# Two-layer hybrid encoder: attention weighed with values as the stationary operand, group weights broadcast through memory, four gates computed last, scan steps paced one by one

## The chip, the cores and the metric

One core of a Trainium2 chip runs the whole program. The metric is the device time of one execution in microseconds (us), the median of three runs. PE is TensorE's matmul side and PEld its weight loads, DVE is VectorE, ACT is ScalarE, POOL is GpSimd, SP is SyncE, whose queue issues most of the transfers.

## The reference, cut to what matters

Each of the two layers is a half-step feed-forward block, a mixer and another half-step feed-forward block, on 512 positions of 1024 channels. The mixer adds three gated branches:

```
h = rmsnorm(x);  P = h @ W_in
A = gated DeltaNet, 4 heads of 128, both directions, chunks of 64   # a scan over 8 chunks
B = pooling, 4 channel groups, windows 2/4/8/16, a 128x128 map per group
C = 3 groups of 4 heads of 64, dilated windowed attention;          # o_g, lse_g for each group g
    wts = softmax over g of lse_g;  C = sum_g wts_g * o_g           # per position and head
x = x + W_o( sum_i sigmoid(h W_g_i + b_g_i) * (branch_i @ P_i) )
```

## The kernel before

Activations lie with channels on partitions and the 512 positions along the free side. A `gemm` makes 128 output channels: for each of its k-tiles of 128 input channels it runs three matmuls of 128x512 (weights and activations are each split into a high and a low part, `wh`/`wl` and `h`/`l`; the three products are lines 232, 234 and 236). Weights come by DMA on SP's queue into `raw` (three buffers), ACT copies `wh` and DVE subtracts `wl` (`split`, lines 182 and 183, four buffer pairs). A gemm on the normed input has 8 k-tiles, 24 matmuls; the projections of branches A and B (`wpa`, `wpb`) have 12 and that of branch C (`wpc`) has 6. Three PSUM banks hold gemm results (`acc`), five hold everything else (`m`).

The mixer is a row of gemms into which smaller work is threaded. `step()` is called after every gemm matmul, and two lanes count these calls: lane "d" releases a piece of the DeltaNet every 14 calls (`DPACE`), lane "a" a piece of attention every 13 or 9 calls (the numbers in `ORDER`). A chunk of the scan is `read` (16 matmul records, then eight DVE instructions, line 679), `solve` (line 699, then lines 706 and 708) and `write` (line 716, then line 726); each needs the one before it. A scheduler with priorities then fixes the order on each engine, and every engine runs its own queue in order.

`ORDER` runs the projections of attention group 0, its attention, groups 1 and 2, the pooling branch in one piece, then the eight `wpa` gemms (`y`) with the attention of group 2 among them, then `merge`. Attention works on blocks of four softmax tiles of 128 queries: `scores`, softmax, `turn` (four transposes of the probabilities into `pe`, lines 899 and 902) and `weigh` (line 914): `pe`, 128x128, is the stationary operand and 64 columns of values move past it, so the result has queries on partitions. `merge` therefore multiplies each group's result by a column of weights (line 961), transposes it on PE (line 966, 24 transposes) and adds the three. It writes group 0's weights to memory and reads them back in another order (lines 954 and 956).

Then come eight `wpb` and eight `wpc` gemms. The gates of branches B and C were computed early and stored to memory (`gd`); each gemm loads its gate tile (line 1086, on ACT's queue, four buffers `f`), DVE forms the product (line 1088) and POOL adds it to `mg[d]` (line 1089). The eight output gemms `wo` need all of `mg`, split into high and low parts.

Of the kernel before, what the change touches and what calls it, by code (L numbers as in the profile page):

```python
# [16 lines left out]
P = 128  # L17
# [79 lines left out]
def trunk(ctx: ExitStack, tc: tile.TileContext, A, out):  # L97
# [69 lines left out]
    dW = pd.tile([T, 4], F32, name="dW")  # L167
    gd = pd.tile([2 * NB, P, T], F32, name="gd")
# [36 lines left out]
    lanes = {"d": [[], 0, DPACE], "a": [[], 0, 0]}  # L205

    def step():

        for ln in lanes.values():
            if ln[0]:  # L210
                ln[1] += 1
                if ln[1] >= ln[2]:
                    ln[1] = 0
                    ln[0].pop(0)()

    def drain(k, left=0):
        while len(lanes[k][0]) > left:
            lanes[k][0].pop(0)()
# [153 lines left out]
    def deltanet(l, W):  # L372
# [175 lines left out]

        for tok in DNORD[1].split():
            {"v": values, "t": vrows, "q": queries, "n": qnorm}[tok[0]](int(tok[1]))  # L550
# [10 lines left out]
        for tok in DNORD[2].split():  # L561
            {"v": values, "t": vrows, "q": queries, "n": qnorm}[tok[0]](int(tok[1]))
        V.tensor_scalar(out=qv, in0=qv, scalar1=4 * L2_EPS, scalar2=None, op0=ALU.add)

# [77 lines left out]
        def krows(h):  # L642
# [10 lines left out]
            KD.append(kd)  # L653

# [89 lines left out]
        def out_norm():  # L744
            v = small(16, "ov", 1)
            V.tensor_scalar(out=v, in0=qv, scalar1=P * RMS_EPS, scalar2=None, op0=ALU.mult)
# [20 lines left out]
        def add(*fs):  # L767
            X.steps.append(lambda: [f() for f in fs])
# [36 lines left out]
    def attention(l, W):  # L805
# [8 lines left out]
        def project(g):  # L814
# [7 lines left out]
            for hp in range(2):  # L822
# [4 lines left out]
                p = bank()  # L827
                if g == 0:
                    p2 = bank()
                    PE.transpose(p[:64, 0:P], vf[:, 0:64], ident)  # L830
                    for s in range(1, 4):
                        PE.transpose(p[:, s * P:(s + 1) * P], vf[:, s * P - 64:s * P + 64], ident)
                    PE.transpose(p2[:64, 0:P], vf[:, 448:512], ident)
                    S.activation(vx[:64, hp * P:(hp + 1) * P], p2[:64, 0:P], AF.Copy)
                    S.activation(vt[:64, hp * P:(hp + 1) * P], p[:64, 0:P], AF.Copy)
                    o3 = vt.rearrange("p (s c) -> p s c", c=256)[:, 1:4, hp * P:(hp + 1) * P]
                    S.activation(o3, p[:, P:T].rearrange("p (s c) -> p s c", c=P), AF.Copy)
                else:
                    for r in range(4):
                        PE.transpose(p[:, r * P:(r + 1) * P], vf[:, r:T:4], ident)  # L840
                    o3 = vt.rearrange("p (s c) -> p s c", c=256)[:, :, hp * P:(hp + 1) * P]
                    S.activation(o3, p.rearrange("p (s c) -> p s c", c=P), AF.Copy)
            qkv[g] = (q, k, vt, vx)

        def attend(g):

            q, k, vt, vx = qkv[g]
            og = OG[g] = ring()
# [359 lines left out]
```

## Time and profile before

| what | value |
|---|---|
| median of 3 runs | 2594.52 us (2593.94 to 2596.76) |
| the profiled execution's own time | 2593.36 us |
| its span, first to last instruction | 2591.6 us |
| PE busy | 2565.7 us, 99% |
| DVE, ACT, POOL busy | 1469.1, 1008.9, 162.3 us |
| granted TensorE clock | 0.998 |

The difference between the execution's time and its span lies outside the instructions. Matmuls are pipelined, so the duration of one is longer than the distance to the next: what a matmul costs is read from the distance between starts.

### The profile page before, as it was taken

To read this page: it belongs to the slowest core of one execution; us is meant where nothing else is said; L and a number is where in the kernel's file an instruction comes from. 1 tells how busy PE (TensorE), PEld (TensorE's weight loads), DVE (VectorE), ACT (ScalarE), POOL (GpSimd) and SP (SyncE) were. 2 spreads that over 40 slices of the span, in tenths; PEclk is the share of its full clock that TensorE was granted. 3 is DMA by queue.
4 is the path that set the end of the run, shared out by engine and by line. 5 is a ranking of instruction groups with operands and counts; after the bars stand their busy time and mean duration, and the time that the engine had idled before them with its cause. 6 is when DMAs were issued, how large, how long until landed. Compare 5 with 4: busy or idle time off the path is not lost.

```text
span 2591.6 us, 34050 instructions
## 1 busy us (share of the span) xinstructions
PE 2565.7 (99%) x13064; PEld 2102.1 (81%) x13064; DVE 1469.1 (57%) x2698; ACT 1008.9 (39%) x1948; POOL 162.3 (6%) x117
## 2 busy tenths in 40 slices
PE   9999999999999999999999999999999999999998
PEld 7888887888887788888888888878888877888887
DVE  6444349956757754444444443599466487544433
ACT  5333234564434333333233332355644343333322
POOL 1000000000230300000000000000012203000010
PEclk9999999999999999999999999999999999999999
DMA  4223333332432522233322333323334325322232
GB/s 154 97 98 96 112 111 98 99 118 87 122 103 74 171 91 96 97 98 96 100 96 94 97 101 114 112 89 106 107 98 121 92 74 175 98 96 94 94 98 82
DMA packets 96979, 269.36 MB, mean 104 GB/s; under 512 B 15664, under 2 KB 20144, under 8 KB 96816
## 3 DMA queue, kind: packets, MB, share of 16 engines
q1 hardware_dynamic: 75280, 229.39, 28.2%
q10 hardware_dynamic: 21536, 37.80, 4.5%
q8 instruction: 102, 1.67, 0.3%
q14 instruction: 61, 0.50, 0.1%
HBM read 243.99 MB, written 16.86 MB: 101 GB/s over the span
## 4 chain that ended last, share of the span: by engine, by line
PE 95%; DVE 2%; ACT 1%; issue 1%; DMA 1%; POOL 0%; SPq 0%; DVEq 0%; ACTq 0%
PE acc L236 29%; PE acc L232 29%; PE acc L234 29%; PE m L914 1%; PE m L672 1%; PE m L699 1%; PE m L716 1%; PE m L735 1%; PE m L899 1%; PE m L869 0%; DMA raw<-in_wo_dram 0%; DVE wl L183 0%; PE m L647 0%; PE m L1023 0%; PE m L608 0%
## 5 line engine op out<-in xcount | busy, mean ns | idle before, releaser
L182 ACT ACTIVATE wh<-raw 128x512 fp32r<-128x512 f32 (+1 forms) x870 | 539.1, 620 | 1193.0 <-PE acc L234 1068.7
L234 PE MATMUL acc<-xl,wh 128*128 128x512 f32 x2400 | 941.9, 393 | 1.4 <-DVE xl L1126 1.2
L236 PE MATMUL acc<-xh,wl 128*128 128x512 f32 x2400 | 941.7, 392 | 1.4 <-DVE wl L183 1.4
L232 PE MATMUL acc<-xh,wh 128*128 128x512 f32 x2400 | 941.1, 392 | 1.3 <-ACT wh L182 1.1
L183 DVE TENSOR_TENSOR wl<-raw,wh 128x512 fp32r<-128x512 f32 (+1 forms) x870 | 606.0, 697 | 578.1 <-ACT wh L182 572.1
L232 PEld LDWEIGHTS acc<-xh,wh 128*128 128x128 f32 x2400 | 450.9, 188 | 99.1 <-issue 3.0
L234 PEld LDWEIGHTS acc<-xl,wh 128*128 128x128 f32 x2400 | 450.9, 188 | 96.9 <-DVE xl L1126 3.9
L236 PEld LDWEIGHTS acc<-xh,wl 128*128 128x128 f32 x2400 | 451.0, 188 | 96.7 <-DVE wl L183 2.3
L232 PE MATMUL acc<-r,wh 128*128 128x512 f32 x970 | 379.8, 392 | 5.8 <-DVE f L1088 4.5
L234 PE MATMUL acc<-r,wh 128*128 128x512 f32 x970 | 378.5, 391 | 3.5 <-DVE r L183 3.5
L236 PE MATMUL acc<-r,wl 128*128 128x512 f32 x970 | 377.7, 390 | 0.0
L232 PEld LDWEIGHTS acc<-r,wh 128*128 128x128 f32 x970 | 182.1, 188 | 46.5 <-ACT r L182 4.4
L234 PEld LDWEIGHTS acc<-r,wh 128*128 128x128 f32 x970 | 182.2, 188 | 42.5 <-DVE r L183 5.8
L236 PEld LDWEIGHTS acc<-r,wl 128*128 128x128 f32 x970 | 182.1, 188 | 37.5
L298 DVE TENSOR_TENSOR t<-acc,R 128x512 f32<-128x512 f32 x88 | 60.9, 692 | 132.2 <-PE acc L236 132.2
L294 DVE TENSOR_TENSOR f<-acc,R 128x512 f32<-128x512 f32 x88 | 60.9, 692 | 128.1 <-PE acc L236 128.0
L182 ACT ACTIVATE r<-t 128x512 fp32r<-128x512 f32 x96 | 60.6, 632 | 132.6 <-DVE t L299 127.4
L183 DVE TENSOR_TENSOR r<-t,r 128x512 fp32r<-128x512 f32 x96 | 66.2, 692 | 60.8 <-ACT r L182 60.8
L579 POOL MEMSET r<- 128x1024 f32 x2 | 1.9, 953 | 1107.7 <-PE acc L236 1107.7
L365 DVE SCALAR_TENSOR_TENSOR f<-t,cw,f 128x512 f32<-128x512 f32 x96 | 69.2, 741 | 0.0
L295 ACT ACTIVATE f<-f 128x512 f32<-128x512 f32 x88 | 55.6, 632 | 23.0 <-DVE f L294 22.9
L299 DVE TENSOR_TENSOR t<-t,f 128x512 f32<-128x512 f32 x88 | 60.4, 686 | 1.3 <-ACT f L295 1.3
(282 smaller groups left out, 1744.6 us busy)
## 6 DMA issues: line engine op xcount, KB each, us to landing
raw<-in_win_dram SPq DMA_DIRECT2D x76, 512.0 KB, 3.7
raw<-in_wgt_dram SPq DMA_DIRECT2D x48, 512.0 KB, 3.3
raw<-in_f2g_dram SPq DMA_DIRECT2D x44, 512.0 KB, 3.2
raw<-in_f2u_dram SPq DMA_DIRECT2D x44, 512.0 KB, 3.3
raw<-in_f1g_dram SPq DMA_DIRECT2D x43, 512.0 KB, 3.3
raw<-in_f1u_dram SPq DMA_DIRECT2D x43, 512.0 KB, 3.3
raw<-in_f1d_dram SPq DMA_DIRECT2D x32, 512.0 KB, 3.5
raw<-in_f2d_dram SPq DMA_DIRECT2D x32, 512.0 KB, 3.4
```

Of the source, the lines that this page charges most:

```text
L182: S.activation(h, raw, AF.Copy)
L183: V.tensor_tensor(out=l, in0=raw, in1=f32(h), op=ALU.subtract)
L232: PE.matmul(acc, a, h, start=(k == 0), stop=False)
L234: PE.matmul(acc, a, l, start=False, stop=False)
L236: last = PE.matmul(acc, b, h, start=False, stop=(k == nk - 1))
L294: V.tensor_tensor(out=g1, in0=g, in1=R, op=ALU.mult)
L295: S.activation(g1, g1, AF.Silu)
L298: V.tensor_tensor(out=u1, in0=u, in1=R, op=ALU.mult)
L299: V.tensor_tensor(out=u1, in0=u1, in1=g1, op=ALU.mult)
L365: V.scalar_tensor_tensor(out=a, in0=cp[:, j:j + T], scalar=w[:, j:j + 1], in1=a, op0=ALU.mult, op1=ALU.add)
L672: PE.matmul(p1[:, h * P:(h + 1) * P], KQ[h][:, c * P:(c + 1) * P], X.ST[:, di * T + h * P:di * T + (h + 1) * P], start=True, stop=True)
L699: PE.matmul(P3[di][r0:r0 + 64, h * P:(h + 1) * P], M[di][r0:r0 + 64, o:o + 64], U[b][r0:r0 + 64, di * T + h * P:di * T + (h + 1) * P], sta ...
```

## The change

- `weigh` takes a pair of blocks (even and odd heads). The values, 128x64, become the stationary operand and the probabilities, 128 columns, move. The two blocks write the two halves of the partitions, so the result has channels on partitions, and the 24 transposes of `merge` go.
- The pieces of lane "a" are fewer: two `turn`s and the next `scores` in one piece, one `weigh` for a pair, a piece every 20 calls (36 before the second). Group 2's attention starts after its projection and the third pooling gemm.
- The group weights are computed with the last `weigh`, transposed once (48x128), written to memory, and read back by six transfers that repeat each row over 64 partitions. `merge` is then seven DVE products and sums on whole tiles, without PE, at high priority.
- Four of the eight branch C gates are no longer stored early: each is computed just ahead of its `wpc` gemm. `gd` shrinks from 16 tiles to 12.
- The scan is paced with 15 calls ahead of `read`, 13 ahead of `solve` and 9 ahead of `write`, in place of 14 each. The squares of the queries (`qnorm`) move into the DeltaNet's lane.
- Pooling is split into four pieces, and the transposes of attention's values (`vrow`) wait until the next piece of a lane that comes at least 8 calls later.

```diff
-DNORD = ("k0 k1 k2 k3 E0 G0 q0 E1 G1 E2", "v0", "v1 t0 t1 v2 t2 v3 t3 n0 q1 n1 q2 n2 q3 n3")
-ORDER = "p0 a0/13 p1 p2 D a1/9 P D a2/9 y D m"
+DNORD = ("k0 k1 k2 k3 E0 G0 q0 E1 G1 E2", "v0", "v1 t0 t1 v2 t2 v3 t3 q1 q2 q3")
+
+ORDER = "p0 a0 p1 P0 P1 a1 p2 P2 a2 P3 y"
+APACE = 20
+DUE = 8
+
+NG = 4
+YORD = "10 11 12 13 14 15 16 17 20 21 22 23 24 25 26 27"
 MG = 13
-DPACE = 14
+DPACE = {"read": 15, "solve": 13, "write": 9}
...
-    dW = pd.tile([T, 4], F32, name="dW")
-    gd = pd.tile([2 * NB, P, T], F32, name="gd")
+    dW = pd.tile([48, P], F32, name="dW")
+    gd = pd.tile([NB + NG, P, T], F32, name="gd")
...
-    lanes = {"d": [[], 0, DPACE], "a": [[], 0, 0]}
+    lanes = {"d": [[], 0], "a": [[], 0]}
+
+    pend = []
+
+    def flush(due=0):
+        while pend and pend[0][0] >= due:
+            pend.pop(0)[1]()
 
     def step():
 
+        for q in pend:
+            q[0] += 1
         for ln in lanes.values():
             if ln[0]:
                 ln[1] += 1
-                if ln[1] >= ln[2]:
+                if ln[1] >= ln[0][0][0]:
                     ln[1] = 0
-                    ln[0].pop(0)()
+                    flush(DUE)
+                    ln[0].pop(0)[1]()
...
             KD.append(kd)
+            qnorm(h)
...
             if s:
-                add(lambda s=s: read(s))
-            add(lambda s=s: solve(s))
+                add(lambda s=s: read(s), n=DPACE["read"])
+            add(lambda s=s: solve(s), n=DPACE["solve"])
             if s == 5:
-                add(lambda: write(5), lambda: out_block(1), lambda: out_block(2))
+                add(lambda: write(5), lambda: out_block(1), lambda: out_block(2), n=DPACE["write"])
             elif s < 7:
-                add(lambda s=s: write(s))
-        X.rest = 4
+                add(lambda s=s: write(s), n=DPACE["write"])
+        X.rest = 5
         add(lambda: out_block(0), lambda: out_block(3))
         add(out_norm)
+        add()
...
+                pend.append([0, lambda hp=hp, vf=vf: vrow(g, hp, vf, vt, vx)])
...
-            def weigh(b, y):
-                if b.ip not in po:
-                    po[b.ip] = bank()
-                i, h, s, n = b.ks[y]
-                t_ = i + s
-                vv = vx[:n, h * 64:h * 64 + 64] if t_ == 4 else vt[:n, t_ * 256 + h * 64:t_ * 256 + h * 64 + 64]
-                o_ = (i - b.ip) * 256 + h * 64
-                PE.matmul(po[b.ip][:, o_:o_ + 64], b.pe[:n, y * P:(y + 1) * P], vv, start=(s == 0), stop=(s == kw // P - 1))
+            def weigh(pair):
+                if g not in OG:
+                    flush()
+                    OG[g] = ring()
+                og = OG[g]
+
+                ip = pair[0].ip
+                if ip not in po:
+                    po[ip] = bank()
+                for y in range(4):
+                    for b in pair:
+                        i, h, s, n = b.ks[y]
+                        t_ = i + s
+                        vv = vx[:n, h * 64:h * 64 + 64] if t_ == 4 else vt[:n, t_ * 256 + h * 64:t_ * 256 + h * 64 + 64]
+                        o_ = (h // 2) * 256 + (i - ip) * P
+                        PE.matmul(po[ip][64 * b.par:64 * b.par + 64, o_:o_ + P], vv, b.pe[:n, y * P:(y + 1) * P], start=(s == 0), stop=(s == kw // P - 1))
+                if pair[1] is [c for c in B if c.ip == ip][-1]:
+                    S.activation(og.rearrange("p (f t) -> p f t", f=2)[:, :, ip * P:(ip + 2) * P], po[ip].rearrange("p (f t) -> p f t", f=2), AF.Copy)
...
-            steps = [lambda: scores(pairs[0])]
-            for j, pair in enumerate(pairs):
-                if j + 1 < len(pairs):
-                    steps.append(lambda n=pairs[j + 1]: scores(n))
-                for b in pair:
-                    steps.append(lambda b=b: turn(b))
-                for b in pair:
-                    steps.append(lambda b=b: [weigh(b, y) for y in range(4)])
+
+            def first(j):
+                for b in pairs[j - 1] if j else []:
+                    turn(b)
+                if j < len(pairs):
+                    scores(pairs[j])
+            steps = [lambda: first(0)]
+            for j in range(len(pairs)):
+                steps.append(lambda j=j: first(j + 1))
+                steps.append(lambda j=j: weigh(pairs[j]))
+            if g == 2:
+                last = steps.pop()
+                steps.append(lambda: [weights_a(), last(), weights_b()])
...
-            nc.sync.dma_start(dW.rearrange("(m r) h -> m r h", r=4), we[:, 0:16].rearrange("p (r h) -> p r h", h=4))
-            w0 = small(16, "w0", 1)
-            nc.sync.dma_start(w0.rearrange("p (b h) -> p b h", h=4), dW.rearrange("(b p) h -> p b h", p=P))
-            for g in (1, 2, 0):
-                wcol = w0 if g == 0 else we[:, 16 * g:16 * g + 16]
-                V.tensor_tensor(out=OG[g].rearrange("p (x d) -> p x d", d=64), in0=OG[g].rearrange("p (x d) -> p x d", d=64),
-                                in1=bc(wcol, 64), op=ALU.mult)
-                for f in range(2):
-                    p = bank()
-                    for i in range(4):
-                        PE.transpose(p[:, i * P:(i + 1) * P], OG[g][:, i * 256 + f * P:i * 256 + (f + 1) * P], ident)
-                    if g == 0:
-                        V.tensor_tensor(out=yc[f], in0=p, in1=yc[f], op=ALU.add)
-                        continue
-                    yv = yc[f].rearrange("p (m r) -> p r m", r=4)
-                    pv = p.rearrange("p (r m) -> p r m", r=4)
-                    if g == 1:
-                        S.activation(yv, pv, AF.Copy)
-                    else:
-                        V.tensor_tensor(out=yv, in0=pv, in1=yv, op=ALU.add)
+            wp = WT_p[0] = small(48, "wp", 1)
+            for g in range(3):
+                V.tensor_tensor(out=wp[:, 16 * g:16 * g + 16].rearrange("p (h r) -> p r h", r=4),
+                                in0=we[:, 16 * g:16 * g + 16].rearrange("p (r h) -> p r h", h=4),
+                                in1=zz[:, 0:16].rearrange("p (r h) -> p r h", h=4), op=ALU.mult)
+
+        WT_p = [None]
+
+        def weights_b():
+
+            pw_ = bank()
+            PE.transpose(pw_[:48, 0:P], WT_p[0], ident)
+            wr = tt()
+            S.activation(wr[:48, 0:P], pw_[:48, 0:P], AF.Copy)
+            nc.sync.dma_start(dW, wr[:48, 0:P])
+            for g in range(3):
+                w = ring()
+                WT.append(w)
+                for e_ in range(2):
+
+                    src = dW[16 * g:16 * g + 16, :].rearrange("(f e r) m -> e f (r m)", f=2, e=2)[e_:e_ + 1]
+                    nc.sync.dma_start(w[64 * e_:64 * e_ + 64, :].rearrange("p (f t) -> p f t", f=2), src.to_broadcast([64, 2, T]))
+
+        def merge():
+            wT = WT
+            for g in (1, 2):
+                V.tensor_tensor(out=OG[g], in0=OG[g], in1=wT[g], op=ALU.mult)
+            V.tensor_tensor(out=OG[1], in0=OG[1], in1=OG[2], op=ALU.add)
+            yc = []
+            for f in range(2):
+                o = OG[0][:, f * T:(f + 1) * T].rearrange("p (m r) -> p m r", r=4)
+                for op, z in ((ALU.mult, wT[0]), (ALU.add, OG[1])):
+                    V.tensor_tensor(out=o, in0=o, in1=z[:, f * T:(f + 1) * T].rearrange("p (r m) -> p m r", r=4), op=op)
+                yc.append(OG[0][:, f * T:(f + 1) * T])
...
-        pw2 = tt()
-        nc.sync.dma_start(pw2, A["poolw"][l])
-        YB = []
-        for g, win in enumerate((2, 4, 8, 16)):
+
+        def pool(g):
+            win = (2, 4, 8, 16)[g]
+            pw2 = small(P, "pw2", 1)
+            nc.sync.dma_start(pw2, A["poolw"][l][:, g * P:(g + 1) * P])
...
-        for d in range(2 * NB):
+        for d in range(NB + NG):
...
-                lanes["a"][0].extend(attend(int(tok[1])))
-                lanes["a"][1:] = [0, int(tok[3:])]
-            elif tok == "D":
-                drain("a")
-            elif tok == "P":
-                YB = pooling(l, W[16:20])
-            elif tok == "m":
-                YC = merge()
+                lanes["a"][0].extend((APACE + 16 * (j == 1), f) for j, f in enumerate(attend(int(tok[1]))))
+            elif tok[0] == "P":
+                YB.append(pool(int(tok[1])))
...
-        for br, yy, wp in ((0, YB, "wpb"), (1, YC, "wpc")):
-            for d in range(NB):
-                t = tf()
-                nc.scalar.dma_start(t, gd[br * NB + d])
-                y = gemm(A[wp][l][d], yy)
-                V.scalar_tensor_tensor(out=t, in0=t, scalar=1.0, in1=y, op0=ALU.add, op1=ALU.mult)
-                G.tensor_tensor(out=mg[d], in0=mg[d], in1=t, op=ALU.add)
+        YC = None
+        for br, d in [(int(c[0]), int(c[1])) for c in YORD.split()]:
+            if br == 2 and YC is None:
+                drain("a")
+                with tc.high_priority(offset=AHEAD_E):
+                    YC = merge()
+            yy, wp = ((YB, "wpb"), (YC, "wpc"))[br - 1]
+            t = tf()
+            if br == 2 and d >= NG:
+                gate(2, d, t)
+            else:
+                nc.scalar.dma_start(t, gd[(br - 1) * NB + d])
+            y = gemm(A[wp][l][d], yy)
+            V.scalar_tensor_tensor(out=t, in0=t, scalar=1.0, in1=y, op0=ALU.add, op1=ALU.mult)
+            G.tensor_tensor(out=mg[d], in0=mg[d], in1=t, op=ALU.add)
```

On PE, at the end of the `wpa` gemms: `m` is a PSUM bank, `acc` a gemm's bank, `r` under line 914 first the probabilities and then the values. Before:

```order
L236 MATMUL acc_7226<-r_5794,wl_7228 128x512
L914 MATMUL m_7217<-r_6560,r_7071 128x64 x4
L232 MATMUL acc_7226<-r_5842,wh_7227 128x512
L234 MATMUL acc_7226<-r_5842,wh_7227 128x512
L236 MATMUL acc_7226<-r_5842,wl_7228 128x512
L232 MATMUL acc_7226<-r_5853,wh_7227 128x512
L234 MATMUL acc_7226<-r_5853,wh_7227 128x512
L236 MATMUL acc_7226<-r_5853,wl_7228 128x512
L966 MATMUL m_7274<-ident,r_6657 128x128 x4
L966 MATMUL m_7280<-ident,r_6657 128x128 x4
L966 MATMUL m_7287<-ident,r_6990 128x128 x4
```

After (line 939 is `weigh`, 246 to 250 the gemm), the same place:

```order
L939 MATMUL m_7107<-r_6945,r_6609 64x128
L939 MATMUL m_7107<-r_6954,r_6609 64x128
L939 MATMUL m_7107<-r_6945,r_6609 64x128
L939 MATMUL m_7107<-r_6954,r_6609 64x128
L939 MATMUL m_7107<-r_6945,r_6609 64x128
L939 MATMUL m_7107<-r_6954,r_6609 64x128
L939 MATMUL m_7107<-r_6945,r_6609 64x128
L939 MATMUL m_7107<-r_6954,r_6609 64x128
L996 MATMUL m_7117<-ident,wp_7103 48x128
L250 MATMUL acc_7071<-r_5851,wl_7073 128x512
L246 MATMUL acc_7071<-r_5862,wh_7072 128x512
```

The operands have changed places, the pieces of the last pair stand together, and one transpose of 48 rows stands where 24 of 128 stood.

On DVE, from the first product of the merge. Before (the `wpa` and `wpb` stages; 961, 975 and 968 are the merge, 183 the splits, 1082 and 1088 the gated products):

```order
L961 TENSOR_TENSOR r_6657<-r_6657,we_7256 128x1024
L183 TENSOR_TENSOR wl_7345<-raw_7346,wh_7344 128x512
L902 COPY r_7071<-m_7194 128x512
L1082 SCALAR_TENSOR_TENSOR mg_3961<-mg_3961,acc_7169 128x512
L1082 SCALAR_TENSOR_TENSOR mg_3999<-mg_3999,acc_7201 128x512
L183 TENSOR_TENSOR wl_7368<-raw_7369,wh_7367 128x512
L961 TENSOR_TENSOR r_5941<-r_5941,w_1301_7270 128x1024
L961 TENSOR_TENSOR r_6990<-r_6990,we_7256 128x1024
L1082 SCALAR_TENSOR_TENSOR mg_4037<-mg_4037,acc_7226 128x512
L183 TENSOR_TENSOR wl_7391<-raw_7392,wh_7390 128x512
L975 TENSOR_TENSOR r_7272<-m_7287,r_7272 128x4x128
L975 TENSOR_TENSOR r_7272<-m_7293,r_7272 128x4x128
```

After (1017, 1011 and 1012 are the merge, 188 the splits, 1137 the gated products of `wpb`):

```order
L1017 TENSOR_TENSOR r_5993<-r_5993,r_7122 128x512 x2
L1137 SCALAR_TENSOR_TENSOR f_7182<-f_7182,acc_7184 128x512
L188 TENSOR_TENSOR wl_7278<-raw_7279,wh_7277 128x512
L1137 SCALAR_TENSOR_TENSOR f_7205<-f_7205,acc_7207 128x512
L188 TENSOR_TENSOR wl_7301<-raw_7302,wh_7300 128x512
L1011 TENSOR_TENSOR r_6568<-r_6568,r_7125 128x1024
L1137 SCALAR_TENSOR_TENSOR f_7228<-f_7228,acc_7230 128x512
L188 TENSOR_TENSOR wl_7337<-raw_7338,wh_7336 128x256
L1011 TENSOR_TENSOR r_6999<-r_6999,r_7128 128x1024
L1137 SCALAR_TENSOR_TENSOR f_7251<-f_7251,acc_7253 128x512
L1012 TENSOR_TENSOR r_6568<-r_6568,r_6999 128x1024
L188 TENSOR_TENSOR wl_7354<-raw_7355,wh_7353 128x256
```

The merge's instructions now stand among the gated products and weight splits of the `wpb` stage, and the last two of them are operands of the first `wpc` gemm.

On SP's queue, the weight loads of the `wpc` stage after the change (before, eight `wpc` loads stood in a row, then the `wo` loads):

```order
L204 DMA raw_7389<-in_wpc_dram 128x256
L204 DMA raw_7405<-in_wgt_dram 128x1024
L204 DMA raw_7442<-in_wpc_dram 128x256
L204 DMA raw_7458<-in_wgt_dram 128x1024
L204 DMA raw_7495<-in_wpc_dram 128x256
L204 DMA raw_7511<-in_wgt_dram 128x1024
L204 DMA raw_7548<-in_wpc_dram 128x256
L204 DMA raw_7564<-in_wgt_dram 128x1024
L204 DMA raw_7601<-in_wpc_dram 128x256
```

A gate's load now stands between two `wpc` loads.

## Rows read from the trace of the kernel before

**Rows 1.** the page, part 4: chain of work that ended last, by engine

```profile
PE 95%; DVE 2%; ACT 1%; issue 1%; DMA 1%; POOL 0%; SPq 0%; DVEq 0%; ACTq 0%
```

**Rows 2.** timeline of PE, `weigh` now (start us, us, what, xcount)

```profile
770.70 0.39 PE L232 MATMUL acc<-xh,wh 128*128 128x512 f32 x1
...
772.61 0.40 PE L236 MATMUL acc<-xh,wl 128*128 128x512 f32 x1
...
836.15 0.39 PE L234 MATMUL acc<-r,wh 128*128 128x512 f32 x1
836.38 1.00 PE L914 MATMUL m<-r,r 128*128 128x64 f32 x8
...
837.51 0.39 PE L232 MATMUL acc<-r,wh 128*128 128x512 f32 x1
```

**Rows 3.** timeline of PE, a `krows` piece of the DeltaNet

```profile
560.95 0.39 PE L232 MATMUL acc<-xh,wh 128*128 128x512 f32 x1
561.27 1.09 PE L647 MATMUL m<-ident,r 128*64 128x128 f32 x16
...
562.63 0.40 PE L236 MATMUL acc<-xh,wl 128*128 128x512 f32 x1
```

**Rows 4.** timeline of PE, the transposes of `merge`

```profile
849.17 2.78 PE L966 MATMUL m<-ident,r 128*128 128x128 f32 x24
851.71 0.47 PE L232 MATMUL acc<-r,wh 128*128 128x512 f32 x1
```

**Rows 5.** windows: stretch, length, busy (xcount) by engine, clock, DMA share, GB/s

```profile
851.71:873.58 21.87, 21.87 (x99) 18.11 (x98) 13.43 (x20) 5.09 (x10) 10.14 (x7) 1.00 0.46 130
873.58:902.00 28.42, 23.63 (x98) 17.55 (x97) 23.58 (x32) 11.54 (x22) 13.62 (x9) 1.00 0.71 235
...
2157.44:2186.00 28.56, 24.04 (x100) 17.91 (x99) 23.88 (x33) 11.97 (x22) 13.58 (x9) 1.00 0.74 236
```

**Rows 6.** waits of PE, whole program: total us, times, longest

```profile
PE acc L232 <- DVE f L1088: 4.5, 4, 1.3
PE acc L234 <- DVE r L183: 3.5, 4, 1.0
...
PE m L899 <- ACT r L889: 1.5, 2, 0.8
```

**Rows 7.** timeline of DVE, merge, `wpb` and `wpc` stages

```profile
846.92 1.22 DVE L961 TENSOR_TENSOR r<-r,w 128x1024 f32<-128x1024 f32 x1
...
860.78 0.69 DVE L183 TENSOR_TENSOR wl<-raw,wh 128x512 fp32r<-128x512 f32 x1
...
863.76 1.74 DVE L183 TENSOR_TENSOR wl<-raw,wh 128x512 fp32r<-128x512 f32 x1 [0.17 <-ACT wh L182]
...
875.20 0.69 DVE L1088 SCALAR_TENSOR_TENSOR f<-f,acc 128x512 f32<-128x512 f32 x1 [0.34 <-issue]
```

**Rows 8.** timeline of POOL, the same stages

```profile
863.67 1.28 POOL L1089 TENSOR_TENSOR mg<-mg,f 128x512 f32<-128x512 f32 x1 [1.05 <-DVE f L1088]
...
874.60 5.80 POOL L1089 TENSOR_TENSOR mg<-mg,f 128x512 f32<-128x512 f32 x4 [1.31 <-DVE f L1088]
```

**Rows 9.** groups by line and shape: busy us, mean ns, idle before

```profile
L801 DVE TENSOR_TENSOR r<-acc,r 128x512 f32<-128x512 f32 x24 | 22.7, 946 | 4.9 <-ACT f L794 4.9
...
L840 PEld LDWEIGHTS m<-ident,f 128*128 128x128 f32 x32 | 4.5, 209 | 2.6 <-DVE f L826 2.6
```

**Rows 10.** timeline of SP's queue, group 0's weights on their way to memory

```profile
841.49 0.33 SPq L954 DMA_DIRECT2D dW<-we  x1
```

**Rows 11.** timeline of DVE, two steps of the scan

```profile
620.28 0.90 DVE L679 SCALAR_TENSOR_TENSOR r<-m,nsc,r 64x128 f32<-64x128 f32 x3
...
637.45 0.68 DVE L708 TENSOR_TENSOR r<-m,Dc 64x512 f32<-64x512 f32 x1
```

**Rows 12.** timeline of PE, what follows on them

```profile
621.39 1.09 PE L699 MATMUL m<-r,r 64*64 64x128 f32 x16
...
639.78 1.16 PE L716 MATMUL m<-r,r 64*128 64x128 f32 x16
```

More of the change, by code (lines that the diff above doesn't have):

```diff
@@ L549, in deltanet @@
         for tok in DNORD[1].split():
-            {"v": values, "t": vrows, "q": queries, "n": qnorm}[tok[0]](int(tok[1]))
+            {"v": values, "t": vrows, "q": queries}[tok[0]](int(tok[1]))
         Lc = [ring(), ring()]
@@ L561, in deltanet @@
         for tok in DNORD[2].split():
-            {"v": values, "t": vrows, "q": queries, "n": qnorm}[tok[0]](int(tok[1]))
-        V.tensor_scalar(out=qv, in0=qv, scalar1=4 * L2_EPS, scalar2=None, op0=ALU.add)
+            {"v": values, "t": vrows, "q": queries}[tok[0]](int(tok[1]))
         for hf in range(2):
@@ L745, in out_norm @@
             v = small(16, "ov", 1)
+            V.tensor_scalar(out=qv, in0=qv, scalar1=4 * L2_EPS, scalar2=None, op0=ALU.add)
             V.tensor_scalar(out=v, in0=qv, scalar1=P * RMS_EPS, scalar2=None, op0=ALU.mult)
@@ L765, in out_head, with add @@
             YA.append((r[:, 0:T], r[:, T:2 * T]))
-        def add(*fs):
-            X.steps.append(lambda: [f() for f in fs])
+        def add(*fs, n=14):
+            X.steps.append((n, lambda: [f() for f in fs]))
         add(lambda: first(0), fill)
@@ L826, in project @@
                     V.tensor_tensor(out=vf, in0=acc, in1=R, op=ALU.mult)
-                p = bank()
-                if g == 0:
[L829 to L837, printed above, removed]
-                else:
[L839 to L842, printed above, removed]
@@ L843, in project, with vrow @@
-            qkv[g] = (q, k, vt, vx)
+                pend.append([0, lambda hp=hp, vf=vf: vrow(g, hp, vf, vt, vx)])
+            qkv[g] = (q, k, vt, vx)
+        def vrow(g, hp, vf, vt, vx):
+            p = bank()
+            if g == 0:
+                p2 = bank()
+                PE.transpose(p[:64, 0:P], vf[:, 0:64], ident)
+                for s in range(1, 4):
+                    PE.transpose(p[:, s * P:(s + 1) * P], vf[:, s * P - 64:s * P + 64], ident)
+                PE.transpose(p2[:64, 0:P], vf[:, 448:512], ident)
+                S.activation(vx[:64, hp * P:(hp + 1) * P], p2[:64, 0:P], AF.Copy)
+                S.activation(vt[:64, hp * P:(hp + 1) * P], p[:64, 0:P], AF.Copy)
+                o3 = vt.rearrange("p (s c) -> p s c", c=256)[:, 1:4, hp * P:(hp + 1) * P]
+                S.activation(o3, p[:, P:T].rearrange("p (s c) -> p s c", c=P), AF.Copy)
+            else:
+                for r in range(4):
+                    PE.transpose(p[:, r * P:(r + 1) * P], vf[:, r:T:4], ident)
+                o3 = vt.rearrange("p (s c) -> p s c", c=256)[:, :, hp * P:(hp + 1) * P]
+                S.activation(o3, p.rearrange("p (s c) -> p s c", c=P), AF.Copy)
@@ L905, in turn @@
                         V.tensor_copy(pe[:n, y * P:(y + 1) * P], pT[:n, y * P:(y + 1) * P])
[L907 to L917 removed]
+            def weigh(pair):
[15 more added lines that the diff above has]
+                    S.activation(og.rearrange("p (f t) -> p f t", f=2)[:, :, ip * P:(ip + 2) * P], po[ip].rearrange("p (f t) -> p f t", f=2), AF.Copy)
+                    if g == 0 and ip == 2:
@@ L930, in attend @@
-            return steps
-        def merge():
+            def first(j):
[10 more added lines that the diff above has]
+                steps.append(lambda: [weights_a(), last(), weights_b()])
@@ L934, in merge, with weights_a @@
+            return steps
+        WT = []
+        def weights_a():
             s0 = small(32, "s0", 1)
@@ L1022, in pooling @@
             p = bank()
-            PE.matmul(p, pw2[:, g * P:(g + 1) * P], o, start=True, stop=True)
+            PE.matmul(p, pw2, o, start=True, stop=True)
             r = ring(F32R)
@@ L1064, in mixer @@
         project, attend, merge = attention(l, W[20:38])
+        pool, YB = pooling(l, W[16:20]), []
         for tok in ORDER.split():
```

18 lines of the change are left out of this document (4 added, 14 removed).

## The prediction

> **What bounds the kernel now.** I read the page's chain of waits first. PE holds 95% of the chain that ended last [rows 1] and the table has it busy for 2565.7 of 2591.6 us, so a stage's time is the number of PE instructions in it times the distance between their starts, plus what PE waits. The windows give that distance: the eight `wpb` gemms, 96 matmuls, take 21.87 us, 0.228 each, with nothing lost [rows 5]. The list of PE's waits is short and names one place above all: the gated products of `wpc` and the splits of `mg` (4.5 and 3.5 us), and then a softmax that was late (1.5 us) [rows 6]. Two things can therefore pay: fewer or shorter PE instructions, and the end of the mixer. The reader should see that no other engine needs to become faster, but that DVE may become late if work moves onto it where PE has no other work.
>
> **The values as stationary operand.** The cost of a piece is taken between fixed gemm matmuls ahead of and behind it, so that slow entries and exits are in it. A `weigh` of one block (8 records) takes 837.51 - 836.15 = 1.36, less two gemm distances 0.46: 0.90 us. Blocks with a 64-key tile take 772.61 - 770.70 = 1.91 - 0.46 = 1.45 us [rows 2]. There are 32 blocks in two layers, 8 of them with such tiles: 24 x 0.90 + 8 x 1.45 = 33.2 us. The trace has no `weigh` in the new form, but it has its shape: `krows` loads a 128x64 stationary operand, moves 128 columns, and alternates between the two halves of the output partitions. Its 16 records take 562.63 - 560.95 = 1.68 - 0.46 = 1.22 us [rows 3]; a pair of blocks is 16 records too. I take this for 12 pairs, and for the four with 64-key tiles add what such tiles cost now, 1.45 - 0.90 = 0.55: 12 x 1.22 + 4 x 1.77 = 21.7 us. Gain **11.5 us**. Bounds: nothing, if the halves do not overlap and a pair stays at 2 x 0.90; 13.7 if the 64-key tiles cost no extra.
>
> **The merge.** The 24 transposes hold PE from 849.17 to 851.71, 2.54 us a layer [rows 4]; in their place is one transpose, 2.54 / 24 = 0.1 us. Gain **4.9 us** in two layers. The group weights are now written to memory after the last `weigh`; six transfers of 256 KB then repeat them over the partitions. Today's shorter trip, from the issue at 841.49 [rows 10] to the product at 846.92 [rows 7], is 5.4 us, and its cover is gemms. The new one has eight `wpb` gemms, 21.9 us, as cover, and the first product that needs weights stands behind the sixth weight split of that stage. The added 1.6 MB in 21.9 us is 72 GB/s on top of 130; the stage after it moves 235 today [rows 5]. I take no cost; without cover it would be some 5.4 us a layer.
>
> **The end of the mixer.** Eight `wpc` gemms (48 matmuls) and the first `wo` gemms follow. From 873.58 to 902.00, 97 matmuls start (98 less one still running): 97 x 0.228 = 22.1 of 28.42 us, so 6.3 us are lost; in the second layer (98.5 starts) 6.1 [rows 5]. The mechanism: a `wpc` gemm is over in 6 x 0.228 = 1.37 us, POOL needs 5.80 / 4 = 1.45 us for a sum [rows 8], and each gate tile has to be loaded into a buffer that POOL must free first, while weights for `wo` are fetched: DMA share 0.71 [rows 5]. So products, sums and splits are late in turn. After the change four `wpc` gemms are separated by 24 gate matmuls, 5.5 us each, and four of the eight loads and eight stores are gone. Behind the last `wpc` gemm come product (0.7), sum (1.5), ACT's and DVE's split (1.3), some 3.7 us with handovers; the first `wo` gemm reaches the last k-tile after 21 x 0.228 = 4.8 us. I leave 0.5 us a layer: gain **11.4 us**, bounds 0 (all of it returns) and 12.4. The four gates cost the same where they now stand.
>
> **What the merge costs on DVE.** Between the end of the first `wpb` gemm and the first `wpc` gemm, 7 x 12 x 0.228 = 19.1 us, DVE must do six gated products and four splits of weights at 0.69 [rows 7], three half-width splits (taken as 0.4), four products and sums in a strided view, for which a strided product now takes 0.95 [rows 9], three on 1024 columns at 1.22, and the two final splits at 0.69 [rows 7]: 4.1 + 2.8 + 1.2 + 3.8 + 3.7 + 1.4 = 17.0. That fits with 2.1 us to spare. But POOL works at the same time. The split at 860.78 takes 0.69 and the one at 863.76, started while POOL's sum ran, takes 1.74: 1.05 more [rows 7, 8]. Six sums fall into the stretch, so 0 to 6.3 us come on top. With four collisions DVE is 4.2 - 2.1 = 2.1 us late. What is late next is the first `wpc` gemm; behind these instructions on DVE also wait the products of the last `wpb` gemms, whose banks the third next gemm needs. I take 2 us a layer, **-4 us**; bounds 0 and 6.3 - 2.1 = 4.2 a layer.
>
> The product at 875.20 reads PSUM and SBUF and keeps its 0.69 under a sum of POOL's [rows 7, 8]. [...]
>
> **Smaller edits.** The delayed value transposes: their weight loads waited 2.6 us for DVE, in part beside PE's work [rows 9]; 8 gemm calls, 1.8 us, now lie between. Gain 1.5 (0 to 2.6). The new attention pace puts 40 calls, 9.1 us, between `scores` and `turn`: the 1.5 us of late softmax [rows 6] go. Against this, group 2's softmax, the last pooling piece, the small weight arithmetic and `wpa`'s products now share DVE around the `wpa` gemms. I allow 1 us a layer, -2 in all; bounds 0 and 4, by twice the 0.8 us that such a wait was at most [rows 6], rounded up, a layer. `qnorm` moves the same instructions. The pooling weights come in four loads, covered by the gemms ahead.
>
> **The scan** does not get shorter by its pace, since PE does the same work; it could only start to wait. `solve` has the least room: DVE ends at 620.28 + 0.90 = 621.18 and PE starts at 621.39, 0.21 us, and one call less takes 0.23. `write` has 639.78 - 638.13 = 1.65, and five calls less take 1.14 [rows 11, 12]. I take nothing; bounds 0 and 3 us.
>
> **Sum.** 11.5 + 4.9 + 11.4 + 1.5 + 1.5 - 4 - 2 = 24.8 us. From the profiled execution's 2593.36 that gives 2568.6. The median is 1.2 above that execution: **2569.7 us**.
>
> **The rivals.** (a) *DVE becomes the bound* around the merge: six collisions instead of four a layer (4.4 worse), the `wpa` stage at its bound (2 worse) and the scan at its bound (3 worse): about 2579. For it: every merge instruction has two SBUF inputs. Against: much of the stage's DVE work reads PSUM. Chance 0.17. (b) *The new `weigh` gains nothing*, so the change does not do what it says: 11.5 worse, 2581. For it: the shape is only known from `krows`, whose moving operand is the identity. Against: the distance does not depend on what the numbers are. 0.06. (c) *More than I take*: no stall at the merge, none at `wpa`, the 64-key tiles free: 24.8 + 6 + 2.2 = 33, 2561.5. For it: the collisions need POOL to start first. 0.14. (d) *The scan's shorter steps make it slower*: each of 44 reads, solves and writes in two layers then waits. It decides from 25 / 44 = 0.57 us a step on; at 0.7 us the time is 2569.7 + 31 = 2600. For it: the 0.21 us of `solve`, and the rotary products of group 0 now fall into the scan's last chunks. Against: the 0.51 left for `write` and the longer `read`. 0.03. (e) The gains at the end come back as a wait for late group weights, about 2592, within the bound: 0.02. My forecast has 0.58.
>
> **How the numbers follow.** The likeliest case gives 2569.7; its own range is 2563 to 2577. The range that leaves out no more than 2 in 10 takes in (c) and most of (a) and (b): 2557 to 2583. This kernel's runs differ by about 0.1%, and 0.2%, 5.2 us, is what I call a difference. Faster: the forecast, (a), (b) and (c), 0.95; same 0.02, from (e); slower 0.03, from (d).
>
> **What would show it.** In the profile after: pieces of `weigh` of 16 records, about 1.0 us long; no transposes in `merge`; windows over the `wpc` and `wo` stages at 0.228 a matmul; PE's waits without the gated products, but with a wait of about 2 us for a split of the merged result ahead of the first `wpc` gemm; splits and merge products on DVE at their usual length plus 1.05 where POOL runs. I am wrong if a pair's `weigh` takes 1.8 us, if that wait is over 4 us, or if PE waits in the scan.

## The result

| | before | after |
|---|---|---|
| median | 2594.23 us (2593.23 to 2596.76, 4 runs) | 2611.44 us (2605.19 to 2612.28, 4 runs) |
| ratio, 95% interval | | 1.006 [1.0042, 1.0077] |
| span of the profiled execution | 2591.6 us | 2609.8 us |

The change makes the kernel 0.6% slower. I forecast 2569.7 us, in a range of 2557 to 2583, and gave slower 3 in 100. PE has fewer instructions and is busy longer, 2588.0 us against 2565.7. Table of engines and chain by engine, from the page of after; the second row answers to [rows 1]:

```profile
PE 2588.0 (99%) x13018; PEld 2090.8 (80%) x13018; DVE 1477.1 (57%) x2702; ACT 1003.2 (38%) x1946; POOL 164.1 (6%) x117
...
PE 97%; DVE 1%; DMA 1%; issue 1%; ACT 0%; POOL 0%; SPq 0%; ACTq 0%; DVEq 0%
```

PE's waits in after, the whole program, against [rows 6]:

```profile
PE acc L246 <- ACT r L187: 6.0, 2, 3.7
...
PE acc L248 <- DVE r L188: 1.5, 2, 0.7
```

The stalls of `wpc` and `wo` and the late softmax are gone; a wait for the split of the merged result has come, longer than forecast, but by itself far too short for the 42 us between forecast and result. So the time is not in a wait. Windows of PE show where it is. They are from a stretch that the change does not touch, the first FFN: its up and gate gemms (100 to 200 us; they read `xh` and `xl`) and its down gemms (325 to 365 us; they read `r` tiles). Before:

```profile
100.00:200.00 100.00, 100.00 (x443) 1.00 0.28 95
325.00:365.00 40.00, 40.00 (x178) 1.00 0.35 109
```

After:

```profile
100.00:200.00 100.00, 100.00 (x430) 1.00 0.28 92
325.00:365.00 40.00, 40.00 (x178) 1.00 0.32 97
```

In the same 100 us, with PE busy throughout and the same granted clock, 430 matmuls start in place of 443. In the down gemms it is 178 in both. So the matmuls that read `xh` or `xl` have become slower, and those that read `r` have not. Between starts, over the whole trace (from one gemm matmul to the next, distances of 200 to 300 ns), `xh`/`xl` matmuls go from 227.4 to 232.7 ns on average, `r` matmuls stay at 226.9. The program has 7232 of the first kind: 7232 x 5.3 ns = 38 us.

The instructions are the same. What differs is where tiles lie. The three edits of the pool of small tiles (`pw2`, 512 bytes a partition; `wp`, 192; less `w0`, 64) push all later pools up by 640 bytes, the weight buffers among them, while `xh` and `xl`, declared earlier, stay. From the two built programs, in bytes of the partition:

```
          xh0     wh (first)  wh - xh0      r (first)   r - wh
before    24064   79104       215   x 256   112896      132 x 256
after     24064   79744       217.5 x 256   113536      132 x 256
```

Theory: a matmul is slower when its weights do not lie a multiple of 256 bytes away from its moving tile. Rivals: the weights' own address, the granted clock (0.996 on average in after, 0.998 before), or the changed order of work.

### The profile page after: what moved, and what is told of

Its sections match the earlier page's. It is cut to its first block, busy times and chain, and to the rows that moved or that the text cites. A ratio compares the mean times of both kernels' runs of the same rounds, so it can differ in the third digit from the quotient of the medians.

```text
span 2609.8 us, 33951 instructions
## 1 busy us (share of the span) xinstructions
PE 2588.0 (99%) x13018; PEld 2090.8 (80%) x13018; DVE 1477.1 (57%) x2702; ACT 1003.2 (38%) x1946; POOL 164.1 (6%) x117
## 4 chain that ended last, share of the span: by engine, by line
PE 97%; DVE 1%; DMA 1%; issue 1%; ACT 0%; POOL 0%; SPq 0%; ACTq 0%; DVEq 0%
PE acc L250 30%; PE acc L246 29%; PE acc L248 29%; PE m L685 1%; PE m L939 1%; PE m L886 1%; PE m L712 1%; PE m L729 1%; PE m L748 1%; PE m L916 1%; DMA r<-dW 0%; PE m L659 0%; PE m L1067 0%; DVE wl L188 0%; PE m L620 0%
## 5 line engine op out<-in xcount | busy, mean ns | idle before, releaser
L248 PE MATMUL acc<-xl,wh 128*128 128x512 f32 x2400 | 951.7, 397 | 2.4 <-DVE xl L1175 2.4
L246 PE MATMUL acc<-xh,wh 128*128 128x512 f32 x2400 | 952.2, 397 | 1.2 <-DVE t L375 0.9
L250 PE MATMUL acc<-xh,wl 128*128 128x512 f32 x2400 | 953.0, 397 | 0.4 <-DVE wl L188 0.4
```

The source lines that it names most:

```text
L246: PE.matmul(acc, a, h, start=(k == 0), stop=False)
L248: PE.matmul(acc, a, l, start=False, stop=False)
L250: last = PE.matmul(acc, b, h, start=False, stop=(k == nk - 1))
```

## Experiments on the placement

Moving the weights means here: the weight buffers and all pools behind them.

**Weights of the changed kernel 128 bytes further up.**

```diff
         ffn(A["f2g"][l], A["f2u"][l], A["f2d"][l], xs, None if last else 3 * l + 3, False)
+    pc.tile([P, 32], F32, name="pad2")
```

> The changed kernel with 128 bytes per partition of unused tile declared last in the pool of small tiles: the weight buffers and all that lies behind them move up by 128 bytes, nothing else changes. Theory (distance between the addresses of the stationary and the moving operand): the weights are then a multiple of 256 bytes away from xh and xl, as they were before the change, the starts of the 7232 gemm matmuls that read xh or xl go from 232.7 ns apart on average back to 227.4, and the time falls by 7232 x 5.3 ns = 38 us to about 2573. Rival (the lower granted clock of the changed kernel, 0.996, or its other order of work slows the gemms): no change, 2611.

Measured: 2572.0 us, ratio to before 0.9915 [0.9901, 0.9928]. An unused tile takes 39 us off the changed kernel, about what was expected here, and the time now lies in the range of the prediction. Its PE in the same window, with the mean granted clock of the run at 0.997:

```profile
100.00:200.00 100.00, 100.00 (x442) 1.00 0.29 95
```

**All of it moved together.**

```diff
-    pc.tile([P, 8], F32, name="pad")
+    pc.tile([P, 40], F32, name="pad")
```

> The changed kernel with the same 128 bytes put ahead of xh and xl instead (the existing pad grows from 8 to 40 numbers), so that xh, xl, the weights and everything behind move together. Theory (the distance between the two operands): it stays 128 above a multiple of 256, and the time stays at about 2611. Rival (the weights' own address decides): the weights lie where the first experiment puts them, and the time falls to about 2573.

Measured: 2609.89 us, 1.0061 [1.0047, 1.0075]; 232.6 ns. The weights lie where the experiment ahead put them, and nothing is gained: it is the distance, not the address.

**The kernel before, weights moved by 128, by 256 and by 64 bytes** (the first experiment's tile, of 32, 64 and 16 numbers).

> The kernel before with 128 bytes of unused tile declared last in the pool of small tiles, which makes the distance between weights and xh 128 above a multiple of 256. Theory: the 7232 matmuls come 5.3 ns later each, about 2594 + 38 = 2632, with distances that alternate between 229 and 237 ns in the first FFN. Rival (the loss belongs to the changed code): 2594.

Measured: 2629.55 us, 1.0137 [1.0123, 1.0151]. The kernel before loses 36 us to one unused tile. Same window:

```profile
100.00:200.00 100.00, 100.00 (x430) 1.00 0.28 93
```

> The kernel before with 256 bytes of unused tile in the same place. Theory (the distance modulo 256 decides): nothing changes, 2594. Rival (any other placement than the one before is slower, or the period is longer than 256 bytes): slower, up to 2632.

Measured: 2594.5 us, 1.0003 [0.9994, 1.0012].

> The kernel before with 64 bytes of unused tile declared last in the pool of small tiles: the weights then lie 64 above a multiple of 256 bytes away from xh and xl. Theory A (a conflict that depends on how the two streams of addresses stand to each other within 256 bytes): between the two cases seen, the mean distance of matmuls that read xh or xl is over 228 ns and the time between 2600 and 2632. Theory B (only the offset of 128 collides, as with two banks): 2594. Nothing measured so far tells them apart.

Measured: 2634.46 us, 1.0159 [1.0144, 1.0175]; 233.3 ns. Theory B falls. Theory A's mean distance holds, and its range of time is passed by 2 us: 64 bytes cost 41 us, 128 bytes 36. Of the offsets tried, 0 and 256 are free, 64 and 128 are not; between or beyond them nothing was tried.

**Only `wl` moved against `wh`**, to see whether it is the weight load at all.

```diff
+        h = pw.tile([P, WK * P], F32R, tag="wh", name=nm("wh"))
+        if not gap:
+            gap.append(pw.tile([P, 32], F32, tag="gap", bufs=1, name="gap"))
+        return h, pw.tile([P, WK * P], F32R, tag="wl", name=nm("wl"))
```

> The kernel before with 128 bytes of unused tile between the wh and the wl buffers. Then wh is a multiple of 256 bytes from xh and xl and 128 off from the r tiles, wl is 128 off from xh and xl and a multiple of 256 from the r tiles. Theory (the weight load that runs beside a matmul's stream of columns collides with that stream by their distance, whatever the tiles are called): of the three weight loads of a k-tile one collides in gemms on xh and xl, two in gemms on r, so the gemms on r, which were never slow so far, become slower too: about 7232 x 5.3 / 3 + 3042 x 5.3 x 2 / 3 = 13 + 11 us, 2618. Rival (it is something of xh, xl and the small tiles against the rest, not the weights): gemms on r keep 227 ns, and the time is 2594 or 2632.

Measured: 2636.88 us, 1.0169 [1.0153, 1.0184]. The gemms on `r` are slow for the first time, 233.3 ns. PE in the two windows, the second of them the down gemms with 173 starts in place of 178:

```profile
100.00:200.00 100.00, 100.00 (x434) 1.00 0.30 95
325.00:365.00 40.00, 40.00 (x173) 1.00 0.32 97
```

The direction is as expected, the size is not: 43 us, where I had 24. The timeline of PE shows why (lines 237, 239 and 241 are here the three matmuls of a k-tile; first gemms on `xh` and `xl`, then on `r`):

```profile
149.67 0.39 PE L237 MATMUL acc<-xh,wh 128*128 128x512 f32 x1
149.89 0.40 PE L239 MATMUL acc<-xl,wh 128*128 128x512 f32 x1
150.12 0.40 PE L241 MATMUL acc<-xh,wl 128*128 128x512 f32 x1
150.36 0.39 PE L237 MATMUL acc<-xh,wh 128*128 128x512 f32 x1
...
329.93 0.39 PE L237 MATMUL acc<-r,wh 128*128 128x512 f32 x1
330.16 0.40 PE L239 MATMUL acc<-r,wh 128*128 128x512 f32 x1
330.39 0.40 PE L241 MATMUL acc<-r,wl 128*128 128x512 f32 x1
330.63 0.39 PE L237 MATMUL acc<-r,wh 128*128 128x512 f32 x1
```

On `xh` and `xl` the next start follows after 0.22, 0.23 and 0.24 us (227, 232 and 234 ns for most in the first FFN). Only the first is at its old distance: its own weights and those loaded while it runs are both `wh` (in the trace of before the load for the next matmul starts with the one that runs, both at 150.17 us, and takes 0.19). A matmul on `wl`, or with `wl` loaded beside it, is slow. I had counted the load beside it alone. On `r`, `wh` is off and one of the two is always `wh`: all three are slow. Counted so, after the fact, the cost is 7232 x 5.3 x 2 / 3 + 3042 x 5.3 = 42 us, near the 43 measured. So a matmul keeps its 227 ns here only where its own and the next weights both lie a multiple of 256 bytes from its moving tile. Why the distance counts is not shown: the runs hold distances between starts and no access to the memory.

## Experiments on the terms of the forecast

All start from the first experiment's kernel, 2572.0 us, where the placement no longer hides the edits. From the traces, the distances from each PE instruction's start to the next one's, waits included, summed by what the instruction is (us; gemms are the three lines of `gemm`):

| | before | after | after, weights 128 up |
|---|---|---|---|
| `weigh` | 30.4 | 18.9 | 18.9 |
| transposes of the merge, of the weights | 5.1 | 0.1 | 0.1 |
| `turn` | 11.0 | 14.4 | 14.4 |
| `read`, `solve`, `write` of the scan | 55.4 | 55.4 | 55.4 |
| gemms on `r` | 677.8 | 675.0 | 672.7 |
| gemms on `xh`, `xl` | 1672.0 | 1704.4 | 1668.4 |

From the first column to the last these rows give 21.8 us; the spans of the two profiled executions differ by 20.3.

Apart from the placement, the merge is what the forecast had worst. In the trace of after, SP's queue, where the six broadcasts (`r<-dW`) are issued:

```profile
831.83 0.34 SPq L999 DMA_DIRECT2D dW<-t  x1
833.51 0.34 SPq L204 DMA_DIRECT2D raw<-in_wpb_dram  x1
833.96 1.32 SPq L1006 DMA_DIRECT2D r<-dW  x2
...
840.28 0.33 SPq L204 DMA_DIRECT2D raw<-in_wpc_dram  x1
840.66 0.58 SPq L1006 DMA_DIRECT2D r<-dW  x1
843.52 0.34 SPq L204 DMA_DIRECT2D raw<-in_wpc_dram  x1
843.90 1.23 SPq L1006 DMA_DIRECT2D r<-dW  x2
```

DVE, the second product waiting for the last of them:

```profile
846.61 1.23 DVE L1011 TENSOR_TENSOR r<-r,r 128x1024 f32<-128x1024 f32 x1
...
848.35 0.42 DVE L188 TENSOR_TENSOR wl<-raw,wh 128x256 fp32r<-128x256 f32 x1
851.59 1.23 DVE L1011 TENSOR_TENSOR r<-r,r 128x1024 f32<-128x1024 f32 x1 [2.82 <-DMA r<-dW]
...
854.47 1.48 DVE L188 TENSOR_TENSOR wl<-raw,wh 128x256 fp32r<-128x256 f32 x1
...
858.13 1.27 DVE L188 TENSOR_TENSOR r<-r,r 128x512 fp32r<-128x512 f32 x2
```

The split at 854.47 takes 1.06 us longer than its like at 848.35: it started while a sum of POOL's, from 853.49, ran. That is the collision that the forecast priced at 1.05. In the trace of before, fourteen 128x512 splits started while a sum ran and took 0.92 to 1.78 us; ten that a sum only started beside kept 0.68 to 0.69, and so, at 0.67 to 0.69, did the eleven gated products, which read PSUM, that started while a sum ran.

And PE, the last `wpb` matmul and the first of `wpc`:

```profile
853.54 0.39 PE L250 MATMUL acc<-r,wl 128*128 128x512 f32 x1
857.62 0.49 PE L246 MATMUL acc<-r,wh 128*128 128x512 f32 x1 [3.70 <-ACT r L187]
858.86 0.79 PE L248 MATMUL acc<-r,wh 128*128 128x512 f32 x1 [0.74 <-DVE r L188]
859.45 0.63 PE L250 MATMUL acc<-r,wl 128*128 128x512 f32 x1
859.88 0.63 PE L246 MATMUL acc<-r,wh 128*128 128x512 f32 x1
860.30 0.63 PE L248 MATMUL acc<-r,wh 128*128 128x512 f32 x1
```

The broadcasts stand between weight loads, each of which has to wait until one of three buffers is free, so the last is issued 12 us after the write of the weights; the twelve transfers of the two layers then took 1.4 to 7.0 us from issue to landing. Behind the stall the starts are 0.43 us apart. The window has the granted clock at 0.50, after PE had started two matmuls in 5.3 us:

```profile
858.80:862.00 3.20, 3.14 (x7) 0.50 0.37 138
```

In the first experiment's kernel the same place, from the last `wpb` start to the first at full distance:

```profile
842.27 0.39 PE L250 MATMUL acc<-r,wl 128*128 128x512 f32 x1
845.73 0.51 PE L246 MATMUL acc<-r,wh 128*128 128x512 f32 x1 [3.08 <-ACT r L187]
...
850.09 0.40 PE L250 MATMUL acc<-r,wl 128*128 128x512 f32 x1
```

Nine starts in 7.82 us, of which 9 x 0.227 = 2.04 are work: 5.8 us lost. In the second layer it is nine starts from 2115.80 to 2123.18 us, 5.3 us lost. I had forecast 2 a layer.

**The broadcasts ahead of the weight loads on SP's queue.**

```diff
+            with tc.high_priority(offset=AHEAD_E):
                 nc.sync.dma_start(dW, wr[:48, 0:P])
                 for g in range(3):
```

> The changed kernel with the 128 bytes of the first experiment, and in it the write of the group weights and the six broadcast transfers at high priority, so that all six stand on SP's queue ahead of the weight loads that were between them (the place of one wpb load and two wpc loads). Theory (late weights: the last of the six transfers holds DVE 2.40 and 1.92 us ahead of the second product, and the merge is late by what stood between them on the queue): the waits of the first wpc gemm, 4.65 and 4.17 us, fall to under 1 us each, and the time from 2572 to about 2564 to 2566. Rival 1 (DVE is full in this stage, by the splits and POOL's sums): only the 4.3 us of idle time go at most, 2568 to 2572. Rival 2 (the weight loads behind the six transfers become late): 2572 or more.

Measured: 2569.08 us, 0.9907 [0.9892, 0.9922], 2.9 us less than the first experiment, but the intervals of the two ratios overlap. DVE no longer waits for the broadcasts, but the `wpc` loads behind them now come late:

```profile
PE acc L246 <- ACT wh L187: 5.3, 4, 2.4
```

**The broadcasts on ACT's queue.**

```diff
-                    nc.sync.dma_start(w[64 * e_:64 * e_ + 64, :].rearrange("p (f t) -> p f t", f=2), src.to_broadcast([64, 2, T]))
+                    nc.scalar.dma_start(w[64 * e_:64 * e_ + 64, :].rearrange("p (f t) -> p f t", f=2), src.to_broadcast([64, 2, T]))
```

> The same kernel as the first experiment, with the six broadcast transfers issued from ACT's queue in place of SP's. Theory (late weights): as in the one with all six first on SP's queue, if ACT, which waits for the write of the weights and then issues, is not late with its own splits: about 2566. Rival (ACT's waits delay the splits of weights behind them on ACT): over 2572, with waits of PE for wh.

Measured: 2568.43 us, 0.9903 [0.9887, 0.992], 3.6 us less than the first experiment; all four times lie below its lowest. Now the gated products are what PE waits for, 2.2 us a layer at the first `wpc` gemm:

```profile
PE acc L246 <- DVE f L1137: 4.4, 2, 2.2
```

So late weights are some 3 to 4 us of the merge's 11, close to what these runs can tell apart; behind them DVE is full, and PE's wait for it has the size that I had forecast. Of the expectations for the two runs, the one that only DVE's idle time goes is nearest.

**A late gate as cover for the merge.**

```diff
-YORD = "10 11 12 13 14 15 16 17 20 21 22 23 24 25 26 27"
+YORD = "10 11 12 13 14 15 16 17 24 20 21 22 23 25 26 27"
```

> The changed kernel with the 128 bytes of the first experiment, and with one of the four late gates (24 matmuls on xh and xl, 5.5 us) and its wpc gemm moved ahead of the other wpc gemms, so that the gate lies between the last wpb gemm and the first use of the merged result. Theory (the first wpc gemm waits 4.65 and 4.17 us because the merge ends late on DVE, which has no other cover there): 5.5 us of cover take both waits to under 0.5 us, 2572 - 8 = 2564. Rival (the wait comes back behind it, since three gates are left at the end for the sums and splits ahead of wo, and the gate's own weights are split in the full stage): 2568 to 2575.

Measured: 2566.41 us, 0.9893 [0.9879, 0.9906]: the lowest median of all versions, 1.1% under the kernel before, and between the two expectations. The long wait for the merged result is gone (the largest for an `r` of ACT is 1.0 us); shorter ones are left around the gate and the first `wo` gemm:

```profile
PE acc L246 <- ACT r L187: 1.7, 3, 1.0
```

The granted clock stays at 1.00 here in both layers.

**Both.** The two diffs together.

> The same, with the six broadcast transfers on ACT's queue as well. Theory (with the gate as cover the weights' lateness no longer matters, since the waits are gone): the same time as without it, 2564, within 2 us. Rival (DVE, full, then delays the gate's product or the wpc products, and what starts earlier helps): 2 to 4 us less, 2560 to 2562.

Measured: 2577.39 us, 0.9935 [0.9922, 0.9947]. Both expectations miss. DVE now has another order: three gated products of `wpb` stand behind the whole merge (at 843.73 us in the first layer), and PE waits for the banks that they hold. Why the scheduler chose this order was not tested:

```profile
PE acc L246 <- DVE f L1137: 8.0, 2, 4.1
```

Behind the two waits the granted clock is 0.50 for a time, and 16 gemm starts stand about 0.43 us apart. At 0.2 us each that is an estimated 3 of the 11 us lost against the run before; the waits are most of the rest.

**All gates stored early again.**

```diff
-NG = 4
+NG = 8
```

> The changed kernel with the 128 bytes of the first experiment and all eight gates of branch C stored early again (NG = 8): the gates at the end of the mixer are undone alone. Theory of the forecast (the eight wpc gemms in a row outrun POOL's sums and the loads, 6.3 and 6.1 us, and the late gates take that away): about 11.4 us more, 2583, with PE's waits for the gated products and the splits of mg as before the change. Rival (the merge's own wait, which now comes ahead of the wpc gemms, lets DVE and POOL catch up, or the order of the rest hides it): 2572 to 2577.

Measured: 2589.91 us, 0.9984 [0.9975, 0.9993]: 17.9 us more than the first experiment, where I had 11.4. The waits of before are back at the end of the mixer, beside the merge's:

```profile
PE acc L248 <- DVE r L188: 5.4, 4, 2.3
PE acc L246 <- ACT r L187: 4.3, 2, 2.2
PE acc L246 <- DVE f L1137: 3.9, 3, 1.6
```

Not all of the 17.9 us are waits. Behind the merge's stall and again behind those at the end of the mixer the clock falls; here in the first layer:

```profile
868.40:873.90 5.50, 5.50 (x14) 0.50 0.39 117
889.20:894.40 5.20, 5.20 (x13) 0.50 0.64 233
```

In the two layers 41 gemm starts stand about 0.43 us apart, against 12 in the first experiment. The 29 more, at 0.2 us each, are an estimated 6 us, which leaves 12 for the waits themselves, near the 11.4 forecast.

## Why the prediction was wrong

**The step that failed** is the first one: "a stage's time is the number of PE instructions in it times the distance between their starts, plus what PE waits". I took that distance, 0.228, as a constant of the engine, and summed only the parts that the diff touches. It depends on where the two operands lie, and the change moved the weights under 7232 matmuls that it does not touch. New small tiles were costed as their loads, "covered by the gemms ahead". That is an estimated 38 us, shown from both sides: taken out of the changed kernel (-39) and put into the one before (+36). No rival of mine had it.

**The terms themselves** come out at 2593.89 - 2572.0 = 21.9 us against 24.8, read in the first experiment's kernel:
- `weigh`: 11.5 forecast, 11.5 by the table. A piece of a pair, against [rows 2], takes 721.85 - 720.50 = 1.35 us from gemm matmul to gemm matmul in after, about 1.1 without the gemm's own distance; `krows` was the right model: its 16 records take 1.09 us with the identity moving [rows 3], those of `weigh` 1.09 with the probabilities.

```profile
720.50 0.40 PE L248 MATMUL acc<-xl,wh 128*128 128x512 f32 x1
720.82 1.09 PE L939 MATMUL m<-r,r 128*64 128x128 f32 x16
721.85 0.50 PE L250 MATMUL acc<-xh,wl 128*128 128x512 f32 x1
```

- Transposes of the merge: 4.9 forecast, 5.0 measured.
- End of the mixer: 11.4 forecast. The stalls of before are gone: from 850 us to the end of `wo`, and in the same stretch of the second layer, the distances between gemm starts add up to 0.227 us each, so 12.4 are gained. In the stretch with the last late gates and the first `wo` gemms, against [rows 5], PE is never idle:

```profile
869.00:890.00 21.00, 21.00 (x94) 1.00 0.54 176
```

  Undone alone, the late gates cost 17.9, of which an estimated 6 are the lower clock.
- Merge on DVE: -4 forecast, bound -8.4; 5.8 + 5.3 = -11.1 measured. The first layer's wait, 3.70 us and 0.74 behind it in after, is over the 4 us that I had named as a sign of being wrong. Place and mechanism were right, and with the weights in time PE's wait is 2.2 us a layer against my 2. Missed were the weights, late behind other loads on SP's queue (rival (e), to which I gave 2 in 100, since I counted the whole `wpb` stage as their cover), and the lower clock behind the stall.
- The scan, 0: confirmed; its three lines take the same time. The softmax's late waits are gone, as forecast, and so is the wait of the value transposes for DVE (2.6 us before). The wait of 2 us at `wpa` did not come. `turn`, now two blocks in a row ahead of `scores`, takes 3.4 us more, which I had not counted. With the end of the mixer, the merge and the softmax's 1.5 us taken out, the gemms' rows of the table still hold a gain of some 6 us, from fewer pieces between the gemms perhaps; no run separates it. That 2572.0 lies so near to 2569.7 is therefore partly luck: the losses on the merge and on `turn`, 10.5 us more than forecast, are in part made up by what I had not forecast.

## What to carry to other kernels

A forecast made only from the edited instructions assumes that the others keep their pace: compare the tiles' placement in the two programs, above all of a matmul's weights and its moving tile (227 against 233 ns here), before anything else. If untouched matmuls change pace by a few per cent with PE busy throughout, as here from 443 to 430 in 100 us, an unused tile of the size that restores the old distance tells at once: 128 bytes gave 39 us back. And a transfer has as cover only what is left after the queue it stands in has let it go: the last broadcasts were issued 12 us after the write of the weights.

## What the runs showed of the hardware

- Moving tile and weights of 128x512 matmuls in fp32r: 227 ns between starts at a distance of a multiple of 256 bytes, 233 ns at 64 or 128 above one; after shows the latter as an alternation of 229 and 237 ns in the first FFN. Own and next weights both count: with `wl` alone moved, 227 ns on `xh` and `xl` where both are `wh`, 232 and 234 where one is `wl`. Moving both operands together changes nothing (2609.89 against 2611.44 us).
- In the changed kernel a stall of 3.70 us in one piece, with a second behind it, was followed by a granted clock of 0.50 for 6.8 us. The stalls of before, 6.3 us in waits of 1.3 us at most, left it at 1.00 [rows 5, 6]. The length of a stall alone does not tell: with the broadcasts on ACT's queue PE waited 2.2 us in each layer, and the clock fell behind the first wait only (a line of the timeline and a window of each):

```profile
844.80 0.47 PE L246 MATMUL acc<-r,wh 128*128 128x512 f32 x1 [2.20 <-DVE f L1137]
846.20:849.40 3.20, 3.20 (x9) 0.50 0.83 276
...
2116.63 0.47 PE L246 MATMUL acc<-r,wh 128*128 128x512 f32 x1 [2.21 <-DVE f L1137]
2116.00:2120.00 4.00, 3.37 (x15) 1.00 0.58 174
```

- An earlier transfer can cost time: with the gate as cover, broadcasts from ACT's queue made the kernel 11 us slower; the order on DVE changed with them, and the clock fell behind the new waits.
